# Reading the moving operand of a matmul by turns from its two halves, and adding shuffled sums into x with a step

## The chip, the cores and the metric

The kernel runs on 1 core of one Trainium2 chip. The metric is the device time of one execution in microseconds (us). Three runs of the kernel before the change gave 1353.87, 1353.93 and 1354.22 us; their median, 1353.93 us, is the time that the change is held against.

## What is computed

A trunk of four layers works on 256 tokens of width 1024, in float32. Each layer has a mixer (layers 0 and 3 an RWKV-7 mixer, layer 1 stick-breaking attention, layer 2 attention over selected keys), and after it a SwiGLU feed-forward part. Both add into the residual x. Cut to what the change touches:

```python
def swiglu(h, w_gu, w_down):
    g, u = jnp.split(h @ w_gu, 2, axis=-1)
    return (jax.nn.silu(g) * u) @ w_down

for i in range(DEPTH):
    h = rms_norm(x, norm_mix[i])
    ...
    x = x + y            # y = (mixer output) @ w_out, 1024 x 1024
    x = x + swiglu(rms_norm(x, norm_ffn[i]), ffn_w_gu[i], ffn_w_down[i])
return x
```

The feed-forward width is 2816, so one layer multiplies by two matrices of 1024 x 2816 (gate and up) and one of 2816 x 1024 (down).

## The kernel before

**Layout.** Everything is kept transposed: the 128 partitions hold features, the free axis holds the 256 tokens (S = 256). x lives in four tiles `xt[0..3]`, each with two chunks of 128 features, so eight chunks in all (NC = 8).

**Precision by parts.** The large products run in the format that the code calls F32R, four bytes an element. Each operand is split into a high part, which is the value cast to F32R, and a low part, which is the rest. The product is high x high + high x low + low x high. A weight piece of 512 KB (128 partitions x 1024 floats) is loaded by DMA into a `raw` tile; ScalarE (or VectorE) casts it to `wh`, and VectorE subtracts to get `wl` (`piece`). In the feed-forward part some pieces go to places of a tile named `wring` instead of `wh` and `wl`.

**Gate and up** (`gemm1`, called from `ffn`). The activation tile `xg` holds for each of the eight chunks the high part and behind it the low part, 256 columns each and next to one another. Per chunk there are two matmuls into one PSUM bank: `wh` against all 512 columns (high and low at once), and `wl` against the 256 columns of the high part. Columns 256 to 511 of the bank are then added to columns 0 to 255 (`add2`, a ScalarE copy and a VectorE addition). 22 such pieces for gate and 22 for up make 352 pairs of matmuls a layer. The sums are scaled by the reciprocal root mean square (`rstd_bcast`, which holds one value per token in every partition), go through silu, and their product is split again into `h`: high 256 columns, low 256 columns.

**Down** (the second half of `ffn`). For each of the eight output chunks m, 22 pairs of the same kind (512 columns, then 256 columns) are accumulated in one bank `dn`; two VectorE additions of 256 columns then add both halves of the bank into `xt`. That is 176 pairs a layer. In the last layer the last chunk is done in two banks, low parts first.

**Output products of the mixers** (`out_half`). For each of four pairs of chunks, 4 x 2 groups of three matmuls of 256 columns go into a bank `po`, and one VectorE addition of 512 columns adds it into `xt[j]`. It is called twice in each mixer: 192 matmuls a mixer.

**Order.** All operations are recorded and then issued in an order that is stored in the source as a table of numbers (`ORDER`), so every instruction has the line of the recording helper (L564); in the profile, groups are told apart by the names of their tiles. VectorE, ScalarE, TensorE and the DMA queue each work strictly in their stored order.

**Where a step already occurs.** Before the change no matmul reads its moving operand with a step between neighbouring elements: the innermost step is one element throughout. One small copy does: the tile `E` (in `rwkv`) is filled from `SB` by copies of 32 partitions x 512 elements whose innermost step is 128 elements, that is 512 bytes. A few of these run on ScalarE, a few on VectorE. A copy `XT<-XT` of 32 partitions x 1024 elements next to it reads runs of 32 neighbouring elements.

Of the kernel before, what the change touches and what calls it, by code (L numbers as in the profile page):

```python
# [16 lines left out]
F32R = mybir.dt.float32r  # L17
BF16 = mybir.dt.bfloat16
AF = mybir.ActivationFunctionType
ALU = mybir.AluOpType  # L20
# [4 lines left out]
P = 128  # L25
S = 256
D = 1024
NC = D // P
NF = 11
# [311 lines left out]
x=|C=_^-S9$_0-qF-xI@0F%_o6-  # L341
# [29 lines left out]
class Plan:  # L371
# [15 lines left out]
    def unit(self, at_once=1, ns=0.0):  # L387

        plan = self

        class Unit:
            def __enter__(self):
                plan.unit_op = Op("tensor")
                plan.unit_op.ns = ns

            def __exit__(self, *_):
                op, plan.unit_op = plan.unit_op, None
                op.cost /= at_once
                op.cost = op.ns or op.cost
                plan._add(op)  # L400

        return Unit()
# [63 lines left out]
    def after(self, op, preds):  # L466
        op.preds |= set(preds)
# [100 lines left out]
def trunk(ctx: ExitStack, tc: tile.TileContext, xT_in, vecs_in, wts, lora_in, consts_in, id32_in, outT, order, layers=None):  # L568
# [7 lines left out]
    pe, dve, act, pool, sp = (plan.queue(n) for n in ("tensor", "vector", "scalar", "gpsimd", "sync"))  # L576
    anye = plan.queue("any")
    unit = plan.unit

    def T(shape, group=None, name="t", dtype=F32):  # L580
        return plan.tile(sb, [P] + list(shape), dtype, group, name)

    def t1(name):
        return T([S], "t", name)
# [4 lines left out]
    def bank(name, group="ps"):  # L589
        return plan.tile(psum, [P, 512], F32, group, name, "psum")  # L590


    xt = [T([2, S], name=f"xt{j}") for j in range(4)]
    for j in range(4):
        sp.dma_start(xt[j], xT_in[:, 2 * j:2 * j + 2, :])
    onesr = T([P], name="ones", dtype=F32R)
# [42 lines left out]
    def f(ap):  # L639
        return ap.bitcast(F32)  # L640
# [22 lines left out]
    def mm3(out, w, x, start, stop):  # L663
        (wh, wl), (xh, xl) = w, x
        pe.matmul(out, wh, xh, start=start, stop=False)
        pe.matmul(out, wh, xl, start=False, stop=False)
        pe.matmul(out, wl, xh, start=False, stop=stop)

    def split(h, l, src):
        anye.copy(h, src)  # L670
        dve.tensor_tensor(l, src, f(h), op=ALU.subtract)

    def exact(out, w, x, hl):

        split(hl[0], hl[1], x)
        with unit():
            pe.matmul(out, w, hl[0], start=True, stop=False)
            pe.matmul(out, w, hl[1], start=False, stop=True)

    def v3(t, n):  # L680
        return t.rearrange("p (k m) -> p k m", k=n)

    def ab(t):
        return t.rearrange("p (a b) -> p a b", a=2)

    def flat(t):
        return t.rearrange("p a b -> p (a b)")

    def add2(t, o, eng=anye):

        eng.copy(t, o[:, S:])
        dve.tensor_tensor(t, o[:, :S], t, op=ALU.add)

    def gemm1(key, x, name, group="g", raw=None, parts=None):


        out = bank(name, group)
        wh, wl = [v3(t, NC) for t in piece(key, raw, parts)]
        for c in range(NC):
            with unit():  # L700
                pe.matmul(out, wh[:, c], flat(x[:, c]), start=(c == 0), stop=False)
                pe.matmul(out[:, :S], wl[:, c], x[:, c, 0], start=False, stop=(c == NC - 1))
        return out

    def gemm2(key, xs, name):
# [12 lines left out]
    def out_half(key, half, xs, after):  # L718

        for j in range(4):  # L720
            o = bank("po", "g")
            wh, wl = [v3(t, 4) for t in piece(key + (half, j))]
            for k in range(4):
                with unit():
                    for n in range(2):
                        sl = slice(n * P, (n + 1) * P)
                        mm3(o[:, n * S:(n + 1) * S], (wh[:, k, sl], wl[:, k, sl]), xs(k),
                            start=(k == 0 and n == 0), stop=(k == 3 and n == 1))
            dve.tensor_tensor(xt[j], xt[j], ab(o), op=ALU.add)
            if half == 1:  # L730
                after(j)

# [46 lines left out]
        dve.scalar_tensor_tensor(r, a, 1.5, r, op0=ALU.add, op1=ALU.mult)  # L779
        return r  # L780

    def rstd_bcast(summed=False):
        if summed:
            ss = nstate["ss"]
        else:
            ss, sq = bank("ss"), t1("ssq")
            anye.tensor_tensor(sq, nstate["acc"][:, 0], nstate["acc"][:, 1], op=ALU.add)
            exact(ss[:, :S], onesr, sq, [T([S], "t", "ssr", F32R) for _ in range(2)])
        return rsqrt_of(ss[:, :S], S, "rstd", 1.0 / D, eps_rms)

    def rstd_col(rs):
# [8 lines left out]
    def xg_of():  # L800
        x = nstate["xg"]
        return lambda c: (x[:, c, 0], x[:, c, 1])


    def ffn(layer, after):
        last = layer == subs[-1][1]
        x = nstate["xg"]
        rsb = None
        hs = [v.rearrange("p (i k a s) -> p i k a s", i=n, k=2, a=2)
              for v, n in ((T([4096], g, "h", F32R), 4) for g in ("SA", "SZ", "PR"))]  # L810

        ring = T([6, PIECE], "QC", "wring", F32R)

        def place(n):

            return {"parts": ring[:, n // 2 % 3::3] if n % 2 else None}

        for i in range(NF):
            gus = T([2, 2, S], f"s{6 + i % 2}", "gus")
            gs, us = gus[:, 0], gus[:, 1]  # L820
            since = len(plan.ops)
            for k in range(2):
                add2(gs[:, k], gemm1(("g", layer, 2 * i + k), x, "gate", **place(4 * i + k)), act if i >= 0 else anye)
            if i == 0:
                rsb = rstd_bcast()[:, None, :].to_broadcast([P, 2, S])
                plan.ops[-1].haste = HASTE
            dve.tensor_tensor(gs, gs, rsb, op=ALU.mult)
            act.activation(gs, gs, AF.Silu)
            for k in range(2):
                add2(us[:, k], gemm1(("u", layer, 2 * i + k), x, "up", "ps", **place(4 * i + 2 + k)), act if i >= 0 else anye)  # L830
            if i >= 1:
                plan.in_turn(since, "gate", "up")
            dve.tensor_tensor(us, us, rsb, op=ALU.mult)
            dve.tensor_tensor(us, us, gs, op=ALU.mult)
            h = hs[i // 4][:, i % 4]
            act.copy(h[:, :, 0], us)
            dve.tensor_tensor(h[:, :, 1], us, f(h[:, :, 0]), op=ALU.subtract)

        n, since = 0, len(plan.ops)
        for m in range(NC):  # L840
            if last and m == NC - 1:
                o = bank("dn", "g"), bank("dn", "ps")
                ws = {n // NC: (wh, wl)}
                for a in (1, 0):
                    for k in range(2 * NF):
                        i, h = n + k, hs[k // 8][:, k // 2 % 4, k % 2]
                        if i // NC not in ws:
                            ws[i // NC] = [v3(t, NC) for t in piece(("d", layer, i // NC))]
                        wh, wl = ws[i // NC]
                        with unit():  # L850
                            pe.matmul(o[a][:, :S], wh[:, i % NC], h[:, a], start=(k == 0), stop=(a == 1 and k == 2 * NF - 1))
                            if a == 0:
                                pe.matmul(o[a][:, :S], wl[:, i % NC], h[:, 0], start=False, stop=(k == 2 * NF - 1))
                    dve.tensor_tensor(xt[m // 2][:, m % 2], xt[m // 2][:, m % 2], o[a][:, :S], op=ALU.add)
                plan.in_turn(since, "dn")
                after(m // 2, 1)
                continue
            o = bank("dn", "g" if m % 2 else "ps")
            for k in range(2 * NF):
                if n % NC == 0:  # L860
                    wh, wl = [v3(t, NC) for t in piece(("d", layer, n // NC))]
                h = hs[k // 8][:, k // 2 % 4, k % 2]
                with unit():
                    pe.matmul(o, wh[:, n % NC], flat(h), start=(k == 0), stop=False)
                    pe.matmul(o[:, :S], wl[:, n % NC], h[:, 0], start=False, stop=(k == 2 * NF - 1))
                n += 1
            for a in range(2):
                dve.tensor_tensor(xt[m // 2][:, m % 2], xt[m // 2][:, m % 2], o[:, a * S:(a + 1) * S], op=ALU.add)
            if m == NC - 1:
                plan.in_turn(since, "dn")  # L870
            if last and m == NC - 2:
                after(m // 2, 0)
            elif m % 2:
                after(m // 2)
# [500 lines left out]
    def stick(layer, after):  # L1375
# [12 lines left out]
        for p in range(8):  # L1388
            q, k = qk_[:, p, 0], qk_[:, p, 1]
            add2(q, gemm1(("sq", p), x, "qk"))  # L1390
            add2(k, gemm1(("sk", p), x, "qk"))
            if p == 0:
# [388 lines left out]
```

## Time and profile before

| | |
|---|---|
| median of the runs | 1353.93 us |
| span of the profiled execution, first to last instruction | 1351.7 us |
| median less span | 2.2 us |
| mean granted TensorE clock | 1.000 |
| TensorE matmul busy | 1344.5 us, 99% |
| VectorE busy | 1129.5 us, 84% |
| ScalarE busy | 729.8 us, 54% |
| DMA, mean over the span | 164 GB/s |

The median run and the span differ by 2.2 us, which lies outside the first and last instruction. "PE" is TensorE's matmuls and "PEld" its loads of weights, "DVE" is VectorE, "ACT" ScalarE, "SP" the engine that issues the transfers. A matmul's duration in the profile (390 ns, say) is from its start to the end of its results and overlaps the next one. The time that a matmul takes out of the stream is read from the distance between starts, or from the length of a long run of matmuls divided by their number.

The eight large stages, in order of time: the RWKV mixer of layer 0 (to about 185 us), its feed-forward part (to 368), the attention of layer 1 (to 483) and its feed-forward part (to 667), the selected-key attention of layer 2 (to 803), its feed-forward part (to 987), the mixer of layer 3 (to 1165) and the last feed-forward part (to the end). Some names run into one another at the seams.

### The profile page before, as it was taken

How to read it: one execution, taken by the hardware profiler on the slowest of the kernel's cores; microseconds unless marked ns; L12 is line 12 of the kernel's file. 1: busy time of each engine (PE TensorE's matmuls, PEld its weight loads, DVE VectorE, ACT ScalarE, POOL GpSimd, SP SyncE). 2: the span in 40 equal slices, each digit the busy share in tenths (PEclk: the TensorE clock that was granted, in tenths of full speed). 3: DMA queues.
4: the chain of work that ended last, by engine and by line, in shares of the span. 5: the costliest groups of instructions: out<-in, count | busy, mean ns of one | idle time of the engine just before them, and what ended most of it. 6: DMA issues, size and time to landing. Idle time of an engine off the chain costs nothing.

```text
span 1351.7 us, 25734 instructions
## 1 busy us (share of the span) xinstructions
PE 1344.5 (99%) x10388; PEld 1183.0 (88%) x10388; DVE 1129.5 (84%) x1907; ACT 729.8 (54%) x1250; POOL 7.5 (1%) x18
## 2 busy tenths in 40 slices
PE   9999999999999999999999999999999999999998
PEld 8888898888888898888999798888898888988888
DVE  7998899876688899875899989876799997998754
ACT  4945545654344655554256865654148554656532
POOL 0000000000000000000000000000000000000000
PEclk9999999999999999999999999999999999999999
DMA  6422166654564456655646556666644231666554
GB/s 234 162 92 83 50 205 213 197 179 157 190 175 137 140 177 205 208 160 171 201 145 186 155 156 218 199 192 203 189 138 126 98 99 34 215 206 197 176 166 133
DMA packets 62999, 221.89 MB, mean 164 GB/s; under 512 B 7328, under 2 KB 8864, under 8 KB 62624
## 3 DMA queue, kind: packets, MB, share of 16 engines
q1 hardware_dynamic: 62880, 220.25, 52.2%
q8 instruction: 81, 1.33, 0.4%
q14 instruction: 38, 0.31, 0.1%
HBM read 217.08 MB, written 1.05 MB: 161 GB/s over the span
## 4 chain that ended last, share of the span: by engine, by line
PE 99%; DVE 1%; issue 0%; ACT 0%; DVEq 0%
PE gate L564 18%; PE up L564 18%; PE dn L564 18%; PE po L564 7%; PE qk L564 6%; PE vp L564 4%; PE rp L564 3%; PE kp L564 3%; PE vps L564 3%; PE z L564 2%; PE sc L564 1%; PE lora_in L564 1%; PE Y L564 1%; PE cmb L564 1%; PE pg L564 1%; PE attn_o L564 1%
## 5 line engine op out<-in xcount | busy, mean ns | idle before, releaser
L564 DVE TENSOR_TENSOR wl<-raw,wh 128x1024 fp32r<-128x1024 f32 x285 | 347.5, 1222 | 83.4 <-ACT wh L564 80.3
L564 ACT CAST wh<-raw 128x1024 fp32r<-128x1024 f32 x219 | 229.1, 1049 | 171.8 <-PE dn L564 92.8
L564 PE MATMUL dn<-h,wh 128*128 128x512 f32 (+1 forms) x726 | 244.3, 383 | 0.0
L564 PE MATMUL dn<-h,wl 128*128 128x256 f32 x704 | 198.1, 282 | 0.0
L564 PEld LDWEIGHTS dn<-h,wh 128*128 128x128 f32 x726 | 134.7, 188 | 26.9
L564 PE MATMUL up<-xg,wring 128*128 128x512 f32 x704 | 139.9, 336 | 0.0
L564 PE MATMUL gate<-xg,wring 128*128 128x512 f32 x704 | 138.3, 336 | 0.0
L564 PEld LDWEIGHTS dn<-h,wl 128*128 128x128 f32 x704 | 133.0, 189 | 0.0
L564 DVE TENSOR_TENSOR wring<-raw,wring 128x1024 fp32r<-128x1024 f32 x88 | 107.5, 1222 | 27.6 <-ACT wring L564 26.8
L564 PE MATMUL gate<-xg,wh 128*128 128x512 f32 x352 | 126.8, 392 | 0.0
L564 PE MATMUL up<-xg,wh 128*128 128x512 f32 x352 | 126.6, 392 | 0.0
L564 PEld LDWEIGHTS up<-xg,wring 128*128 128x128 f32 x704 | 107.5, 188 | 14.7
L564 PEld LDWEIGHTS gate<-xg,wring 128*128 128x128 f32 x704 | 107.4, 188 | 14.7
L564 ACT CAST wring<-raw 128x1024 fp32r<-128x1024 f32 x76 | 79.9, 1051 | 35.0 <-issue 13.5
L564 PE MATMUL gate<-xg,wl 128*128 128x256 f32 x352 | 98.4, 280 | 0.0
L564 PE MATMUL up<-xg,wl 128*128 128x256 f32 x352 | 98.4, 280 | 0.0
L564 PE MATMUL qk<-xg,wh 128*128 128x256 f32 (+1 forms) x384 | 91.5, 320 | 0.0
L564 PEld LDWEIGHTS up<-xg,wh 128*128 128x128 f32 x352 | 66.1, 188 | 14.5
L564 PEld LDWEIGHTS gate<-xg,wh 128*128 128x128 f32 x352 | 66.1, 188 | 14.4
L564 PE MATMUL qk<-xg,wl 128*128 128x256 f32 x256 | 71.6, 280 | 0.0
L564 ACT COPY gus<-gate 128x256 f32<-128x256 f32 x88 | 32.2, 372 | 71.7 <-PE gate L564 69.7
L564 PEld LDWEIGHTS qk<-xg,wh 128*128 128x128 f32 x384 | 63.6, 188 | 6.2 <-issue 0.5
(322 smaller groups left out, 2656.9 us busy)
## 6 DMA issues: line engine op xcount, KB each, us to landing
raw<-in_wts_dram SPq DMA_DIRECT2D x397, 512.0 KB, 3.8
lora<-in_lora_dram SPq DMA_DIRECT2D x2, 1536.0 KB, 10.6
rhl<-qa SPq DMA_DIRECT2D x32, 64.0 KB, 3.7
xt<-in_xT_dram SPq DMA_DIRECT2D x4, 256.0 KB, 4.1
lora<-in_lora_dram SPq DMA_DIRECT2D x2, 512.0 KB, 6.3
lg<-in_lora_dram SPq DMA_DIRECT2D x8, 128.0 KB, 4.4
inv<-in_id_dram SPq DMA_DIRECT2D x2, 512.0 KB, 3.9
out_dram<-xt SPq DMA_DIRECT2D x3, 256.0 KB, 3.7
```

Source lines behind the costliest of these rows:

```text
L564: getattr(getattr(nc, o.eng), method)(*map(real, args), **{k: real(a) for k, a in kw.items()})
```

## The change

Two new access patterns are brought in. `il` reads 256 columns as 0, 128, 1, 129, 2, 130, and so on: by turns from the first and the second half, with a step of 128 elements (512 bytes) between neighbouring reads. A matmul of 512 columns does that for its high 256 and then its low 256 columns. The matmul's output is written in order, as before, so the tokens stand shuffled in the bank.

- Gate and up (`gemm1` with `il`) read `xg` so. The reciprocal root mean square is made in the same shuffled order, by reading the moving operand of its own two matmuls with `il`; so the products between it, gate and up fit without more work. `h` is then in shuffled order.
- Down reads `h` with `il` once more, so its sums are shuffled twice.
- The output products of the mixers read their moving operand with `il`; their sums are shuffled once.
- The VectorE additions into `xt` undo this: they read the bank with a step of 2 elements (`po`) or 4 elements (`dn`) and write x in token order.

The query, key and value products, the RWKV products `kp`, `rp`, `vp` and the products `z` are left alone. The number, size and order of the instructions on every engine are the same in both programs; what differs is the access patterns, and the line numbers below the new helpers.

```diff
+    def il(t):
+
+        if len(t.cols.shape) == 2:
+            return t.rearrange("p a (q j) -> p a j q", q=2)
+        return t.rearrange("p (q j) -> p j q", q=2)
...
-    def gemm1(key, x, name, group="g", raw=None, parts=None):
+    def gemm1(key, x, name, group="g", raw=None, parts=None, il=lambda t: t if len(t.cols.shape) == 1 else flat(t)):
...
-                pe.matmul(out, wh[:, c], flat(x[:, c]), start=(c == 0), stop=False)
-                pe.matmul(out[:, :S], wl[:, c], x[:, c, 0], start=False, stop=(c == NC - 1))
+                pe.matmul(out, wh[:, c], il(x[:, c]), start=(c == 0), stop=False)
+                pe.matmul(out[:, :S], wl[:, c], il(x[:, c, 0]), start=False, stop=(c == NC - 1))
...
-                        mm3(o[:, n * S:(n + 1) * S], (wh[:, k, sl], wl[:, k, sl]), xs(k),
+                        mm3(o[:, n * S:(n + 1) * S], (wh[:, k, sl], wl[:, k, sl]), [il(x) for x in xs(k)],
...
-            dve.tensor_tensor(xt[j], xt[j], ab(o), op=ALU.add)
+            r = xt[j].rearrange("p n (q j) -> p n q j", q=2)
+            dve.tensor_tensor(r, r, o.rearrange("p (n j q) -> p n q j", n=2, q=2), op=ALU.add)
...
-            exact(ss[:, :S], onesr, sq, [T([S], "t", "ssr", F32R) for _ in range(2)])
+            exact(ss[:, :S], onesr, sq, [T([S], "t", "ssr", F32R) for _ in range(2)], il)
...
+    def quarters(t):
+        return t.rearrange("p (u v) -> p u v", u=4)
+
+    def quartered(o):
+        return o.rearrange("p (v u) -> p u v", u=4)
...
-                    pe.matmul(o, wh[:, n % NC], flat(h), start=(k == 0), stop=False)
-                    pe.matmul(o[:, :S], wl[:, n % NC], h[:, 0], start=False, stop=(k == 2 * NF - 1))
+                    pe.matmul(o, wh[:, n % NC], il(h), start=(k == 0), stop=False)
+                    pe.matmul(o[:, :S], wl[:, n % NC], il(h[:, 0]), start=False, stop=(k == 2 * NF - 1))
...
+            r = quarters(xt[m // 2][:, m % 2])
             for a in range(2):
-                dve.tensor_tensor(xt[m // 2][:, m % 2], xt[m // 2][:, m % 2], o[:, a * S:(a + 1) * S], op=ALU.add)
+                dve.tensor_tensor(r, r, quartered(o[:, a * S:(a + 1) * S]), op=ALU.add)
```

More of the change, by code (lines that the diff above doesn't have):

```diff
@@ L671, in split, with exact @@
         dve.tensor_tensor(l, src, f(h), op=ALU.subtract)
-    def exact(out, w, x, hl):
+    def exact(out, w, x, hl, il=lambda t: t):
         split(hl[0], hl[1], x)
         with unit():
-            pe.matmul(out, w, hl[0], start=True, stop=False)
-            pe.matmul(out, w, hl[1], start=False, stop=True)
+            pe.matmul(out, w, il(hl[0]), start=True, stop=False)
+            pe.matmul(out, w, il(hl[1]), start=False, stop=True)
     def v3(t, n):
@@ L780, in rsqrt_of, with rstd_bcast @@
         return r
-    def rstd_bcast(summed=False):
+    def rstd_bcast(summed=False, il=lambda t: t):
         if summed:
@@ L822, in ffn @@
             for k in range(2):
-                add2(gs[:, k], gemm1(("g", layer, 2 * i + k), x, "gate", **place(4 * i + k)), act if i >= 0 else anye)
+                add2(gs[:, k], gemm1(("g", layer, 2 * i + k), x, "gate", **place(4 * i + k), il=il), act if i >= 0 else anye)
             if i == 0:
-                rsb = rstd_bcast()[:, None, :].to_broadcast([P, 2, S])
+                rsb = rstd_bcast(il=il)[:, None, :].to_broadcast([P, 2, S])
                 plan.ops[-1].haste = HASTE
@@ L829, in ffn @@
             for k in range(2):
-                add2(us[:, k], gemm1(("u", layer, 2 * i + k), x, "up", "ps", **place(4 * i + 2 + k)), act if i >= 0 else anye)
+                add2(us[:, k], gemm1(("u", layer, 2 * i + k), x, "up", "ps", **place(4 * i + 2 + k), il=il), act if i >= 0 else anye)
             if i >= 1:
@@ L850, in ffn @@
                         with unit():
-                            pe.matmul(o[a][:, :S], wh[:, i % NC], h[:, a], start=(k == 0), stop=(a == 1 and k == 2 * NF - 1))
+                            pe.matmul(o[a][:, :S], wh[:, i % NC], il(h[:, a]), start=(k == 0), stop=(a == 1 and k == 2 * NF - 1))
                             if a == 0:
-                                pe.matmul(o[a][:, :S], wl[:, i % NC], h[:, 0], start=False, stop=(k == 2 * NF - 1))
-                    dve.tensor_tensor(xt[m // 2][:, m % 2], xt[m // 2][:, m % 2], o[a][:, :S], op=ALU.add)
+                                pe.matmul(o[a][:, :S], wl[:, i % NC], il(h[:, 0]), start=False, stop=(k == 2 * NF - 1))
+                    r = quarters(xt[m // 2][:, m % 2])
+                    dve.tensor_tensor(r, r, quartered(o[a][:, :S]), op=ALU.add)
                 plan.in_turn(since, "dn")
@@ L863, in ffn @@
                 with unit():
-                    pe.matmul(o, wh[:, n % NC], flat(h), start=(k == 0), stop=False)
-                    pe.matmul(o[:, :S], wl[:, n % NC], h[:, 0], start=False, stop=(k == 2 * NF - 1))
+                    pe.matmul(o, wh[:, n % NC], il(h), start=(k == 0), stop=False)
+                    pe.matmul(o[:, :S], wl[:, n % NC], il(h[:, 0]), start=False, stop=(k == 2 * NF - 1))
                 n += 1
+            r = quarters(xt[m // 2][:, m % 2])
             for a in range(2):
-                dve.tensor_tensor(xt[m // 2][:, m % 2], xt[m // 2][:, m % 2], o[:, a * S:(a + 1) * S], op=ALU.add)
+                dve.tensor_tensor(r, r, quartered(o[:, a * S:(a + 1) * S]), op=ALU.add)
             if m == NC - 1:
```

## The prediction, on record before the changed kernel ran

> **What bounds the kernel now.** First the page's busy shares and its chain, to see which engine sets the end; differences under 0.2% (2.7 us) count below as no change, about what a measurement of this kernel can tell.
>
> ```profile
> span 1351.7 us, 25734 instructions
> PE 1344.5 (99%) x10388; PEld 1183.0 (88%) x10388; DVE 1129.5 (84%) x1907; ACT 729.8 (54%) x1250; POOL 7.5 (1%) x18
> PE 99%; DVE 1%; issue 0%; ACT 0%; DVEq 0%
> PE gate L564 18%; PE up L564 18%; PE dn L564 18%; PE po L564 7%; PE qk L564 6%; PE vp L564 4%; PE rp L564 3%; PE kp L564 3%; PE vps L564 3%; PE z L564 2%; PE sc L564 1%; PE lora_in L564 1%; PE Y L564 1%; PE cmb L564 1%; PE pg L564 1%; PE attn_o L564 1%
> ```
>
> TensorE is the chain for 99% of the span, and the four products that the change touches (gate, up, dn, po) make up 61% of it. So what counts is how long one of their matmuls holds the stream. The chain in order of time gives that from long runs, one of each kind:
>
> ```profile
> 251.51 5.55 PE gate L564 x32
> 257.06 5.55 PE up L564 x32
> 306.98 61.03 PE dn L564 x352
> 1142.22 22.40 PE po L564 x192
> ```
>
> The second column is the length. Gate and up: 5.55 us for 16 pairs, 347 ns a pair. Down: 61.03 us for 176 pairs, 346.8 ns. Output: 22.40 / 192 = 117 ns a matmul of 256 columns. The timeline splits a pair:
>
> ```profile
> 251.70 0.39 PE L564 MATMUL gate<-xg,wh 128*128 128x512 f32 x1
> 251.93 0.28 PE L564 MATMUL gate<-xg,wl 128*128 128x256 f32 x1
> 252.04 0.39 PE L564 MATMUL gate<-xg,wh 128*128 128x512 f32 x1
> ```
>
> From start to start the 512 columns take 0.23 us and the 256 columns 0.11 to 0.12; with 347 for both and 117 from the output row, 230 and 117 ns. Is there anything in this that is not the columns themselves? Two other kinds of 256-column matmuls in this trace tell: the bfloat16 ones that warm the engine up, and the RWKV value product in plain float32.
>
> ```profile
> 6.13 0.49 PE L1615 MATMUL warm_o<-warm_x 128*128 128x256 bf16 x3
> 6.79 1.47 PE L1615 MATMUL warm_o<-warm_x 128*128 128x256 bf16 x12
> ...
> 89.83 1.46 PE L564 MATMUL vp<-xv,raw 128*128 128x256 f32 x6
> ```
>
> ```profile
> L564 PE MATMUL vp<-xv,raw 128*128 128x256 f32 x256 | 57.2, 381 | 0.0
> ```
>
> Three bfloat16 matmuls in a row take 0.49 us and twelve 1.47, so nine more are 0.98 us, 109 ns each. Six float32 ones, less the full duration of one (381 ns in the group's row): (1.46 - 0.38) / 5 = 216 ns, which is twice 108. So 256 columns at one column a beat need 108 to 109 ns, and 512 need 216 to 218. The F32R matmuls, which take four bytes at every beat, need 117 and 230: about 8 ns (256 columns) and 13 ns (512) more. That excess is absent where a column has two bytes (bfloat16) and where a column takes two beats (float32). It isn't the same for all F32R matmuls of one size either; the groups by form differ by the tile that is read:
>
> ```profile
> L564 PE MATMUL dn<-h,wh 128*128 128x512 f32 x682 | 236.9, 390 | 0.0
> L564 PE MATMUL gate<-xg,wh 128*128 128x512 f32 x352 | 126.8, 392 | 0.0
> L564 PE MATMUL vps<-wh,xg 128*128 128x512 f32 x128 | 42.5, 402 | 0.0
> ```
>
> 390, 392 and 402 ns mean for 512 columns out of `h`, `xg` and `wh`. So I read the excess as a stall of the moving operand's read at full rate, and one that depends on where and in which order the addresses come. The order is what the change alters; whether for better or worse this trace doesn't show, as no matmul in it reads with a step.
>
> **The change part by part.**
>
> *The reads of the four products.* Pairs: 4 layers x (352 gate and up + 176 down) = 2112. Output matmuls: 4 mixers x 192 = 768. Bounds on the good side: no excess left at all, a pair of 217 + 109 = 326 ns instead of 347, so 2112 x 21 = 44 us, and 768 x 8 = 6 us; together 50. A floor of another kind stands before that: the next weights have to be loaded within the matmul.
>
> ```profile
> 401.94 0.34 PE L564 MATMUL z<-ehl,ones 128*128 128x128 f32 x2
> 402.05 0.19 PEld L564 LDWEIGHTS qk<-xg,wh 128*128 128x128 f32 x1
> 402.16 0.19 PEld L564 LDWEIGHTS qk<-xg,wl 128*128 128x128 f32 x1
> ```
>
> Behind matmuls of only 128 columns (some 55 ns of columns) two weight loads still start 0.11 us apart, so a load takes about 110 ns of the stream. A 256-column matmul can't fall much under 111. I take 217 + 111 = 328 for the pair: 2112 x 19 = 40 us, and 768 x 6 = 4.6 us for the output.
>
> *Bounds on the bad side* come from the only reads with a step of 512 bytes in this trace, the copies into `E`:
>
> ```profile
> L564 ACT COPY E<-SB 32x512 f32<-32x512 f32 x11 | 12.0, 1090 | 8.3 <-DVE SB L564 8.1
> L564 ACT COPY XT<-XT 32x1024 f32<-32x1024 f32 x2 | 2.1, 1041 | 0.0
> L564 DVE COPY E<-SB 32x512 f32<-32x512 f32 x5 | 3.0, 595 | 0.1
> ```
>
> On ScalarE 512 elements with that step take as long as 1024 in runs (1090 against 1041): half rate. On VectorE they take 595 ns, some 1.1 ns an element. TensorE needs one every 0.42. At half rate a pair costs 2 x 326 = 652 ns: 2112 x 305 = +644 us, and 768 x 99 (216 for 117) = +76. At VectorE's pace a pair would take 768 x 1.1 = 845 ns and an output matmul 282, +1052 and +127 us.
>
> Between -50 and +1180 us I take the value near the good end. The reader of a stream at full rate must already fetch ahead, and the change doesn't alter how many different stretches of memory are read, only that two are open at once, each at half the speed; at half the speed per stretch, plain float32 shows no stall. That is an argument, not a row, and the chances below leave room for the other.
>
> *The additions into x with a step.* 64 and 32 of them:
>
> ```profile
> L564 DVE TENSOR_TENSOR xt<-xt,dn 128x256 f32<-128x256 f32 x64 | 26.6, 418 | 19.9 <-PE dn L564 19.1
> L564 DVE TENSOR_TENSOR xt<-xt,po 128x512 f32<-128x512 f32 x32 | 21.8, 683 | 1.0 <-PE po L564 0.7
> ```
>
> The nearest row with a step on VectorE is the copy into `E` above: 595 ns for 512 elements, less than the 683 here, although its step is far larger. So I take no cost; a gain is out, since one operand and the number of elements stay. Ceiling: half rate for the elements, 418 - 267 = 151 ns fixed, so +0.27 us each and +0.53 for the wide ones: 17 + 17 = 34 us of VectorE, most of it beside TensorE, but two narrow ones stand on the chain where a feed-forward part ends:
>
> ```profile
> 368.03 0.43 DVE xt L564
> 368.49 0.42 DVE xt L564
> ```
>
> That is 4 x 2 x 0.27 = 2 us of the end time at the ceiling.
>
> *The reciprocal root mean square* is two matmuls a layer for the feed-forward parts, a few ns each: nothing.
>
> *What is late next.* VectorE makes the low weights. If TensorE gets faster, VectorE has less time for them. Busy time by stretch (length, PE, PEld, DVE):
>
> ```profile
> 163.00:185.00 22.00, 22.00 (x189) 21.95 (x188) 21.19 (x35) 13.13 (x22) 0.00 (x0) 1.00 0.53 163
> 185.00:240.00 55.00, 55.00 (x320) 48.41 (x319) 53.18 (x79) 31.32 (x53) 0.00 (x0) 1.00 0.68 211
> 240.00:307.00 67.00, 67.00 (x388) 58.98 (x387) 52.54 (x74) 37.62 (x59) 0.00 (x0) 1.00 0.58 181
> 307.00:368.00 61.00, 61.00 (x353) 54.07 (x353) 38.71 (x50) 22.89 (x28) 0.00 (x0) 1.00 0.55 174
> ```
>
> In the second half of gate and up VectorE is at 78%, in down at 63%: room for a stream 5.5% shorter (63.3 and 57.7 us). In the first 55 us of the part it is at 97%: TensorE would need 52.0, VectorE has 53.2 of work there. So 1 to 2 us of the gain are given back in each of four feed-forward parts; I take 4 us in all. In the output product (163 to 185) VectorE is at 96%, so of the 4.6 us I count 2.
>
> Sum: -40 - 2 + 4 = -38 us. Against the profiled execution, 1351.7 becomes 1314; with the 2.2 us outside the span, 1353.9 - 38 = 1316 us.
>
> **The rivals.**
>
> *Only part of it* (0.20). The stall goes for the wide matmuls alone (2112 x 13 = 27 us), or half of it goes (20), or VectorE takes more back: 1328 to 1345, say 1334. For it: the weight floor of 110 is near 117, so the narrow ones may be bound by it already.
>
> *TensorE's pace doesn't change* (0.10). If the stall comes with the bytes and not with their order, the pairs stay at 347 and only the additions are left, 0 to 2 us on the chain: 1354 to 1356, a little more where VectorE is at 97%. Against it: 390 to 402 ns for the same bytes.
>
> *Every read opens a new line* (0.13). [...] It decides as soon as a column of the four products costs more than 347 / 768 = 0.45 ns on average. At half rate the time is 1353.9 + 644 + 76 = 2074 us, at VectorE's pace for such a step 2530. For it: the ScalarE row. Against it: VectorE reads the same pattern at a full element a beat, so the memory itself doesn't force half rate.
>
> [...]
>
> *A small loss* (0.05). The pace stays or gains little, and the additions cost their ceiling in the stretches where VectorE is at 96 to 97%: up to 34 us, 1358 to 1388.
>
> **How the numbers follow.** Forecast, most of the stall gone, 1302 to 1328: 0.52. Faster by over 0.2% is that and the partial case: 0.72. Within 0.2%: 0.07 of the 0.10 for no change of pace. Slower: 0.03 of it, 0.13 and 0.05: 0.21. The low end is 1353.9 - 50, with a little for the reading of the rows: 1302. The high end takes in the partial case, the unchanged pace and the first us of a loss: 1358. What is left out is the line case and most of the small loss, under 0.2.
>
> **What the changed profile would show.** In the chain, runs of 32 gate or up matmuls at 5.25 us (5.55 before) and the down stage at 57.7 (61.03); the mean of a 512-column matmul near 378 ns (390), a 256-column one near 274. Output runs of 192 at about 21.5 (22.40). The `xt` additions at 418 and 683 as before. VectorE over 97% and first TensorE waits for `wl` behind a feed-forward part's start. Wrong: runs of 32 at 5.55 (pace unchanged), or at 10 us and more (the line case, with VectorE's share near 50%); 256-column starts still 117 apart with wide ones shorter (the weight floor); `xt` rows near 690 and 1220.

## The result

The changed kernel takes 1314.39 us (median of four runs, 1313.07 to 1318.03) against 1354.08 for the kernel before (its three runs and a fourth, 1353.87 to 1355.63): a ratio of 0.9707, 95% interval 0.9692 to 0.9722, so 39.7 us or 2.9% less. The forecast was 1316 us. The profiled execution is the slowest of the four, 1318.03 us, with a span of 1316.3.

Page of the changed kernel: span, busy shares, and the chain by engine and by line.

```profile
span 1316.3 us, 25734 instructions
PE 1305.1 (99%) x10388; PEld 1168.9 (89%) x10388; DVE 1126.5 (86%) x1907; ACT 728.3 (55%) x1250; POOL 7.6 (1%) x18
PE 93%; DVE 3%; DMA 2%; ACT 1%; issue 1%; SPq 0%; DVEq 0%; ACTq 0%
```

VectorE's work is the same to 3 us; TensorE's got 39 us less. The chain now leaves TensorE for 7% of the span, where it was 1% before: others have begun to be late.

Chain in order of time, changed kernel (start, length, what): a run of gate, a run of up, a whole down stage, and a run of output products.

```profile
248.90 5.24 PE gate L564 x32
254.14 5.24 PE up L564 x32
...
462.54 10.92 PE po L564 x96
...
589.58 57.64 PE dn L564 x352
```

Gate and up went from 5.55 to 5.24 us for 16 pairs, 327.5 ns a pair; down from 61.03 to 57.64, 327.5 as well. The output products take 10.92 / 96 = 113.8 ns; the same stretch of 96 took 11.40 / 96 = 118.8 before (this row is from the kernel before):

```profile
471.88 11.40 PE po L564 x96
```

The timeline of the changed kernel shows both halves of a pair shorter, 0.21 to 0.22 and 0.11 from start to start:

```profile
245.03 0.27 PE L564 MATMUL up<-xg,wl 128*128 128x256 f32 x1
245.14 0.38 PE L564 MATMUL up<-xg,wh 128*128 128x512 f32 x1
245.35 0.27 PE L564 MATMUL up<-xg,wl 128*128 128x256 f32 x1
```

The groups by form say the same of the durations, and the additions into x with a step cost nothing (changed kernel; the last two rows are from the view of the tile `xt`, durations as minimum, median, maximum):

```profile
L564 PE MATMUL dn<-h,wh 128*128 128x512 f32 x682 | 223.9, 382 | 0.0
L564 PE MATMUL dn<-h,wl 128*128 128x256 f32 x704 | 191.6, 273 | 0.0
```

```profile
L564 DVE TENSOR_TENSOR xt<-xt,dn x64: 412/416/424, 308.7 to 1312.6; 128x256 f32<-128x256 f32 x64
L564 DVE TENSOR_TENSOR xt<-xt,po x32: 676/680/689, 166.9 to 1137.3; 128x512 f32<-128x512 f32 x32
```

What was not gained lies at the start of the feed-forward parts. Between the first gate and the first down matmul 352 pairs at 327.5 ns and two small ones need 115.5 us. By the starts of the first gate and the first down matmul, the first part took 184.52 to 306.82 us before (122.3) and 184.01 to 301.14 now (117.1); the four (117.1, 116.1, 116.8, 117.4) make 467.4 us where 462.0 would do, against 489.3 before. The chain of the changed kernel shows who is late there:

```profile
193.94 5.78 DMA raw<-in_wts_dram
...
199.74 1.05 ACT wh L564
...
203.23 1.23 DVE wring L564
204.45 0.04 issue
204.50 0.38 PE gate L564
```

A weight piece lands, ScalarE casts it, VectorE makes its low part, and only then TensorE goes on. In the view of waits TensorE waits for that by name, which it did nowhere before (total, times, longest):

```profile
PE gate L564 <- DVE wring L564: 0.8, 2, 0.6
```

VectorE's share in the first 56 us of the first feed-forward part is 96% (53.79 of 56.00 us; it was 97% of 55 us before):

```profile
184.00:240.00 56.00, 55.28 (x335) 50.00 (x334) 53.79 (x81) 32.27 (x55) 0.00 (x0) 1.00 0.69 211
```

### The profile page after: what moved, and what is told of

Same layout as the page of the kernel before. It is cut to its first block, busy times and chain, and to the rows that moved or that the text cites. A ratio compares the mean times of both kernels' runs of the same rounds, so it can differ in the third digit from the quotient of the medians.

```text
span 1316.3 us, 25734 instructions
## 1 busy us (share of the span) xinstructions
PE 1305.1 (99%) x10388; PEld 1168.9 (89%) x10388; DVE 1126.5 (86%) x1907; ACT 728.3 (55%) x1250; POOL 7.6 (1%) x18
## 4 chain that ended last, share of the span: by engine, by line
PE 93%; DVE 3%; DMA 2%; ACT 1%; issue 1%; SPq 0%; DVEq 0%; ACTq 0%
PE dn L564 17%; PE up L564 16%; PE gate L564 16%; PE qk L564 6%; PE po L564 6%; PE vp L564 4%; PE kp L564 4%; PE rp L564 3%; PE vps L564 3%; PE z L564 2%; DMA raw<-in_wts_dram 2%; DVE wl L564 1%; PE sc L564 1%; PE lora_in L564 1%; PE Y L564 1%; PE cmb L564 1%
## 5 line engine op out<-in xcount | busy, mean ns | idle before, releaser
L564 PE MATMUL dn<-h,wh 128*128 128x512 f32 (+1 forms) x726 | 230.9, 376 | 0.0
L564 PE MATMUL dn<-h,wl 128*128 128x256 f32 x704 | 191.6, 273 | 0.0
L564 PE MATMUL gate<-xg,wring 128*128 128x512 f32 x704 | 132.8, 328 | 1.3 <-DVE wring L564 0.8
L564 PE MATMUL up<-xg,wring 128*128 128x512 f32 x704 | 133.5, 327 | 0.2 <-DVE wring L564 0.2
L564 PE MATMUL gate<-xg,wh 128*128 128x512 f32 x352 | 121.5, 383 | 0.6 <-DVE xg L564 0.5
L564 PE MATMUL up<-xg,wh 128*128 128x512 f32 x352 | 120.8, 382 | 0.0
L564 PEld LDWEIGHTS up<-xg,wl 128*128 128x128 f32 x352 | 67.6, 192 | 0.3 <-DVE wl L564 0.3
```

The source lines that it names most:

```text
L564: getattr(getattr(nc, o.eng), method)(*map(real, args), **{k: real(a) for k, a in kw.items()})
```

## The experiments

The theory: reading neighbours one after another at full rate stalls the moving operand, and reading two places by turns doesn't; the rest of the kernel only takes a little of that back. The rivals: any shuffle would do; the distance between the halves matters; the stall is a collision with the load of the next weights; the gain is given back by what comes late.

### Ways of reading, measured alone

A kernel that copies x to the output and otherwise only runs 40 matmuls for each way of reading, with 128 x 128 weights, which change every time for F32R (shortened):

```python
("halves",   x[:, 0:256].rearrange("p (q j) -> p j q", q=2))
("quarters", ... q=4)  ("eighths", ... q=8)  ("step16" to "step2", ... q=16 to 128)
("turn2" to "turn32", x[:, 0:256].rearrange("p (q j r) -> p j q r", q=2, r=2 to 32))
("far16b" to "far128b", x[:, 0:256].rearrange("p (j q r) -> p j r q", q=2, r=4 to 32))
("far1k", "far4k", halves of 512 and 2048 elements, 256 columns of them)
```

> This kernel leaves the whole computation out (it copies x to the output) and runs 40 matmuls back to back for each way of reading the moving operand, with weights that change at every matmul, so that the distance between starts is the price of one matmul. If the stall belongs to reading neighbours in turn out of one stretch (my theory), 256 F32R columns in order cost 116 to 118 ns and by turns from two halves 109; more open places (quarters, eighths, steps of 16, 8 and 4 elements) stay at 109 too, and bfloat16 columns cost 109 either way. If two open places are just what a small line store can hold (rival: lines, but two of them), quarters and everything with more places cost more than 117, up to 216. If the shuffling matters only through the distance of the two places (rival: banks), turns at 16, 32, 64 and 128 bytes differ from turns at 512, 1024 and 4096 bytes. If any order that isn't plain neighbours will do, evens then odds (step 2) also costs 109; by my theory it stays at 115 or more, since it walks through one stretch at a time. The same element 256 times costs 109 if the stall comes from moving on to new memory.

Chain of this kernel, one row for each way of 40 (a number at the end of a name is left out by the view: the two `mrun` rows are 256 and 512 columns, the two `mhalves` rows likewise):

```profile
16.67 4.79 PE mrun L65 x40
21.46 4.47 PE mhalves L65 x40
25.93 5.50 PE mquarters L65 x40
31.43 8.93 PE meighths L65 x40
...
106.96 4.47 PE mfar4k L65 x40
111.43 4.47 PE mfar16b L65 x40
...
133.78 9.10 PE mrun L65 x40
142.87 8.63 PE mhalves L65 x40
...
169.01 4.38 PE mbfrun L65 x40
173.40 9.73 PE mbfhalves L65 x40
```

In order, 256 columns cost 120 ns, by halves 112, and 512 columns 227.5 against 215.8. The distance is of no importance: turns between two neighbouring groups of four elements (16 bytes apart) and between places 4 KB apart all cost 112, so the rival of distance falls. Four places cost 137 and eight 223, so "any shuffle" falls too. With it falls much of my own expectation, which had quarters, eighths and the steps of 16, 8 and 4 at 109: the steps of 16 and 8 came at 219 in the mean (17.30 us for 79), the step of 4 at 233. The rival with a store for just two open places had all of these above 117, and was right there. Evens, then odds, walks through one stretch at a time; my theory had it at 115 or more, near the price in order, and it costs twice that. The same element 256 times costs 112, like two places by turns. Cut out of the chain by a window, evens then odds, steps of four (second row) and runs of two by turns (third) read

```profile
66.97 9.08 PE mstep L65 x40
```

```profile
57.66 9.32 PE mstep L65 x40
```

```profile
76.28 6.33 PE mturn L65 x38
```

227, 233 and 167 ns; runs of 4 to 32 by turns cost 128 to 119 (5.11 us for 40, 4.88 for 41). And bfloat16, which I had at 109 either way, costs 243 by halves. So neither the number of stretches alone decides nor how often a new group of four neighbours comes up: in order and by turns between two places that is once in four columns alike, and the prices are 120 and 112. The order in which such groups come up counts, and it counts otherwise in bfloat16 (243 by halves, 109 in order).

### Columns, weights and steps, measured alone

The same frame, with 128 to 512 columns, 32 to 96 weight columns, weights with a step of 8 elements, both places moving on by 2, 4 or 16 elements, and shifted starts.

> This kernel leaves the whole computation out (it copies x to the output) and runs 40 F32R matmuls back to back for each case. In the first pattern run the excess over reading by turns was about the same for 256 columns (120 - 112) and for 512 (227.4 - 215.8), so there are two theories. Mine: the read in order stalls by itself, all along its columns; then the excess grows with the columns from 128 to 512 (by about 3 ns per 128 in order, against none by turns), and stays the same with 32, 64 or 96 weight columns. Rival: it stalls only while the next weights are being loaded, some 110 ns, because both read at once; then the excess is flat from 256 columns on, and shrinks in proportion to the weight columns (12 ns with 128, 3 with 32) with the widest gap for weights read with a step. By either, 128 columns cost about 110 ns with 128 weight columns (the load's own floor) and less with fewer. Two places that each move on by a step of 2 elements tell whether a place serves its neighbours: 112 if two places are enough, 120 or more if a line of 16 bytes has to give four columns in turn; with a step of 4 or 16 elements every read opens a new line: 220 or more. A start shifted by 1, 2, 3, 4 or 8 elements changes little (118 to 122).

Chain of this kernel (`cols` a is 128 columns, c 256, e 384, f 448, g 512; `weights_a` is 32 weight columns, `half` 256 and `full` 512 columns):

```profile
17.25 4.42 PE run_cols_a L66 x40
...
35.09 4.83 PE run_cols_c L66 x40
39.92 4.47 PE turn_cols_c L66 x40
...
55.69 6.94 PE run_cols_e L66 x40
62.63 6.50 PE turn_cols_e L66 x40
69.13 8.27 PE run_cols_f L66 x40
77.40 7.57 PE turn_cols_f L66 x40
...
102.68 4.55 PE run_half_weights_a L66 x40
107.23 4.37 PE turn_half_weights_a L66 x40
111.59 9.27 PE run_full_weights_a L66 x40
120.86 8.64 PE turn_full_weights_a L66 x40
...
192.62 9.61 PE turn_half_stepweights L66 x40
...
221.86 4.80 PE turn_evens L66 x40
226.66 9.07 PE turn_fours L66 x40
...
249.60 5.06 PE shift_two L66 x40
```

With 32 weight columns the excess of reading 512 columns in order is 231.8 - 216 = 16 ns; with 128 it was 11 or 12. So there the collision with the weights' load falls as the cause: a load of a quarter of the size leaves the excess. At 256 columns it doesn't fall altogether. By turns they stand on a floor set by the load: 112 ns with 128 weight columns, about what 128 columns cost (110.5), and 109 with 32. In order they cost 121 and 114. Over the 109, the excess is thus 12 ns with 128 weight columns and 4.5 with 32, near the 12 and 3 that the rival had, though not in proportion (4.5 with 64, 7 with 96). So the read in order has an excess of its own, and at 256 columns a part of it goes with the load.

My half of the expectation isn't borne out cleanly either: the excess doesn't grow evenly (9 ns at 256 columns, 11 at 384, 17.5 at 448, 11 at 512). A shifted start, which I had at 118 to 122, gives 117 (by 3, 4 and 8 elements) to 127 (by 2): the price of the read in order depends on where it starts, and the kernel's 117 lies in this range.

Both places moving on by two elements cost 120, just as much as reading in order; by four, 227, and by sixteen 224 (8.96 us for 40). So the gain is there where each place gives four neighbouring columns, 16 bytes, before it moves on (112, the turns 16 bytes apart above), and gone where each moves on by two elements.

An estimate from these numbers that fits most of them: count, for the even and for the odd columns apart, how often a new group of four elements comes up, and put 1.8 ns on each (227 / 128 for 512 columns in order). In order that is once in four columns, which makes 228 ns for 512 columns and 114 for 256 (231.8 and 114 measured with 32 weight columns); by turns it is once in eight, 114 ns for 512, less than the 215.8 that they take in any case. It fits evens (114 against 120), fours and eighths (227 against 227 and 223) as well. It doesn't fit quarters (137) nor runs of two (167), which it would put at 227, and 448 columns in order take 207 where it has 199. No run shows what stands behind the count; why the order of the reads matters stays open.

### One part of the change at a time

Three kernels, each with one product reading by turns: gate and up with their reciprocal root mean square (`il(h)` back to `flat(h)`, the step of the additions 2 in place of 4, `out_half` as before); down (`gemm1` without `il`, step 2); the output products (the rest as before).

> Only gate, up and their reciprocal root mean square read by turns; down and the output products read in order, and the additions into x undo one shuffle. The traces give 22 us less in the four gate and up stages (5.2 + 6.2 + 5.6 + 4.9) out of 27 that the pace alone would give (1408 pairs x 19.3 ns). My theory (a fixed gain per matmul, less what VectorE and the weight loads take back there): 1354 - 22 = 1332 us. Rival, that the stages share a budget so that the loss in gate and up comes from down and the output products running ahead of their weights: 1327 us, all of the 27.

Measured 1332.42 us (1329.79 to 1335.10), ratio 0.983 with interval 0.980 to 0.986. That is what the theory had, and the whole range lies above the rival's 1327. But two of the four runs had a granted clock of 0.995 and 0.996 (see the last section); the other two took 1329.79 and 1331.44. In the profile of the first of these the four stages take 465.3 us, 24 less than the 489.3 before. So 3.3 us over the 462.0 are given back here too, though down and the output products read in order, which speaks against the rival; the theory's 22 is some 2 us short.

> Only down reads by turns, of an h in token order. 704 pairs x 19.3 ns = 13.6 us; the traces show 3.4 us less in each of four down stages, which had VectorE at 63%, so nothing is taken back: 1354 - 13.5 = 1340.5 us. Rival (the stage is bound by the weight loads, 0.5 MB per 2.6 us): 1344 us or more.

Measured 1342.70 us (1340.59 to 1345.67), ratio 0.991, 0.988 to 0.994. Chain of this kernel:

```profile
602.14 57.64 PE dn L564 x352
```

The stages got their 3.4 us each, as in the full change; the median is 2 us above the forecast, and the best run on it. The profiled run, 1345.67 us, shows where some 5 us went in it: the clock (the last section). At 327.5 ns a pair these stages aren't held up by the weights' transfers, as the rival had it. So this part too is the fixed gain per matmul.

> Only the output products of the mixers read by turns. By the pace alone 768 matmuls x 4 to 8 ns = 3 to 6 us less, 1348 to 1351 us. My theory after seeing the traces: VectorE has 96% work there, the mixers as a whole got only 0.4 us shorter, so 1353.5 us, not to be told from 1354.

Measured 1351.35 us (ten runs, 1350.43 to 1356.09), ratio 0.998, 0.997 to 0.9997. I had it at nothing; alone it brings 2.6 us by the medians, and by the interval 0.4 to 4.2. In the profiles the 768 matmuls are busy for 92.08 us where they read by turns (changed kernel) in place of 95.45, so the pace gives 3.4 us; whether VectorE takes any of that back, these runs can't tell. Chain of this kernel, to 11.40 before:

```profile
471.10 10.92 PE po L564 x96
```

### More open places in the kernel itself

`q=2` becomes `q=4` in `il` and the additions, `u=4` becomes `u=16`.

> The changed kernel, with turns between four quarters in place of two halves (step 64 elements) and the additions into x undoing that. My theory (two open places are read at full rate, four are not): from the patterns alone, 137 ns for 256 columns in place of 112, and twice that for 512, so pairs of 411 ns in place of 327.5: 2112 x 84 = +176 us, and 768 x 24 = +18, about 1508 us. Rival (in the kernel's own mix any shuffle will do): 1314.

Measured 1546.36 us (one run). Chain of this kernel:

```profile
340.46 75.11 PE dn L564 x352
```

A pair takes 427 ns (411 worked out from the patterns; 2112 x 16 ns = 34 of the 38 us above the forecast), so the same kernel with a slightly different shuffle is 14% slower than reading in order. The gain is that of two places, not of shuffling.

### Who takes back the rest

```diff
-            dve.tensor_tensor(gs, gs, rsb, op=ALU.mult)
+            dve.tensor_tensor(gs[:, :, :16], gs[:, :, :16], rsb[:, :, :16], op=ALU.mult)
...
-            dve.tensor_tensor(us, us, gs, op=ALU.mult)
+            dve.tensor_tensor(us[:, :, :16], us[:, :, :16], gs[:, :, :16], op=ALU.mult)
```

> The changed kernel with less work for VectorE in gate and up: the scaling of gate and the product of gate and up are done for 16 of 256 columns of each chunk only (the rest of the output is left wrong), 1.2 us less VectorE work in each of the 44 groups of four pieces. My theory, that VectorE's work on the low weights takes back the missing 6 us in gate and up: the four stages, 117.1, 116.1, 116.8 and 117.4 us, come down to about 115.5 each, 1314 - 5 = 1309 us. Rival, that the weight transfers are late by themselves in the first 40 us of each feed-forward part (the chain has one of 5.8 and one of 5.5 us there): stages and total unchanged, 1314.

The changed kernel was run again beside it:

> The changed kernel again, on the chip of these runs, as the line for the other three: 1314 us, between 1313 and 1318.

Measured 1313.79 us (1312.20 to 1316.24) with less work for VectorE, and 1315.12 (1314.50 to 1316.86) for the changed kernel. VectorE's busy time fell from 1126.5 to 1087.1 us, and the time by 1.3 us where I expected 5; the ranges overlap. In the profiles the first gate and up stage is 299.64 - 183.82 = 115.8 us against 301.38 - 184.72 = 116.7 in the changed kernel's repeat, and its chain there is TensorE alone; but all four stages together are 464.5 against 465.6 us. VectorE's load is thus a part of it at most; how much the landing of the weights does by itself stays open.

### The other products by turns as well

```diff
-mm3(out[:, i * S:(i + 1) * S], (wh[:, c % 4, sl], wl[:, c % 4, sl]), xs(c),
+mm3(out[:, i * S:(i + 1) * S], (wh[:, c % 4, sl], wl[:, c % 4, sl]), [il(x) for x in xs(c)],
...
-add2(q, gemm1(("sq", p), x, "qk"))
+add2(q, gemm1(("sq", p), x, "qk", il=il), turned=True)
...
-pe.matmul(o[tb], xh[:, tsl], wh[:, c % 2, :], start=(c == 0), stop=False)
+pe.matmul(o[tb], xh[:, tsl], il(wh[:, c % 2, :]), start=(c == 0), stop=False)
```

`kp` is treated alike, and the reads of the banks get the step that undoes it.

> The changed kernel, with the remaining F32R products read by turns as well: the query, key and value products of both attentions, and rp and kp of the RWKV mixers; their banks are read back with a step of 2 (by VectorE, and by ScalarE where it copies). By the pace alone: 1272 matmuls of 256 columns x 6 ns = 7.6 us, 128 pairs x 19 ns = 2.4, 192 value matmuls of 512 columns x 16 ns = 3; 13 us below the changed kernel's 1314, so 1301. My theory: the mixers have VectorE at 88 to 97%, so about half of it comes through, 1307 us (1303 to 1311). Rival: ScalarE's and VectorE's reads with a step from PSUM cost as much as they gain, 1314 or more.

Measured 1309.42 us (1308.41 to 1313.78), ratio to before 0.9674, 0.9656 to 0.9693, and 5.7 us under the changed kernel's 1315.12 beside it: faster than both. Chain of this kernel, and then of the changed kernel's repeat:

```profile
364.23 10.58 PE vps L564 x48
375.99 14.14 PE qk L564 x86
```

```profile
365.75 11.41 PE vps L564 x48
378.35 14.96 PE qk L564 x86
```

So 44% of the 13 us by pace came through, within the range expected. That VectorE's load in the mixers took the rest was not tested. Reads of a bank with a step of 2 took as long as without on both engines, so the rival falls: ScalarE's copies from `kp` take 602 against 609 ns and from `qk` 372 in both, VectorE's additions from `qk` 418 against 420. ScalarE's row for `kp` in this kernel:

```profile
L564 ACT COPY k<-kp 128x512 f32<-128x512 f32 x7 | 3.9, 602 | 1.2 <-PE kp L564 1.2
```

## Why the prediction was right

**The bound.** TensorE's stream set the end (99% of the chain before, 93% in the changed kernel), and the price of a matmul in it was what counted. Each of the three parts made alone shortened just its own stages.

**The excess as a stall of the read.** The step that carried the sum, that F32R columns in order cost more than columns by turns, was inferred from rows of other formats and stood without a row of its own. The patterns show it: 120 against 112, 227.5 against 215.8. The reasoning beside it, that two stretches open at once halve the speed of each, holds only in part: by the same reasoning quarters and eighths should have gained too, and they cost 137 and 223 ns; and that the reader fetches ahead is shown by no run. That the change reads two places and not four, which would have made the kernel 14% slower, was luck as far as this argument goes.

**The pair.** Worked out 328 ns, measured 327.5; 2112 x 19.3 = 41 us, against 40. The patterns measured alone add up to it on both sides: 227.5 + 120 = 347.5 ns before and 215.8 + 112 = 327.8 now. The floor by the weights' load, about 110 ns, is there where narrow matmuls follow one another: 128 columns cost 110.5 ns, 256 by turns 112.

**The output products.** 111 ns worked out, 113.8 measured, and 3.4 us by the pace where I had 4.6 and counted 2. Alone it brings 2.6 (0.4 to 4.2). That was right in size; less came from the pace than I had, and that VectorE takes part of it is not shown.

**The additions with a step.** No cost, as taken: 416 and 680 ns against 418 and 683. The ceiling of 34 us was far off. No row shows its 267 ns for 256 elements as it stands; the two rows give 683 - 418 = 265.

**What is given back.** 4 us in the feed-forward starts; the profiles show 5.4 (467.4 - 462.0) in the slowest run and 3.6 (465.6 - 462.0) in the repeat. The place was right: the first TensorE waits for `wring` are there. VectorE's share there is 96%, not over 97%. The cause that I named, VectorE's work on low weights, is at most a part of it, as less of that work gave back some 1 us.

**The rivals.** Not only the wide matmuls gained: those of 256 columns went from 282 to 273 ns in down, and from 118 to 109 from start to start (medians over the trace), so the weights' floor didn't bind them within a pair, and the pace did change. The line case that would have made it 2074 us or more didn't come in for two places. For four it came in part (quarters, 1546 us), and eight cost twice the price (223 ns). No run shows how the reader keeps what it has read, in lines or otherwise; the runs show what an order costs. By turns, where every read is on another group of four elements than the one before, 256 F32R columns cost 112 ns, less than the 120 in order; evens, then odds, which read two elements of a group and then go on to the next, cost 227; and in bfloat16 halves cost 243 against 109. The trace of before couldn't decide that rival, and 0.13 left room for it.

## What to carry to other kernels

Where TensorE is busy all the time, hold the distance between starts against another format's of the same number of columns: an excess of a few per cent in every matmul is worth as much as a long stall (here 347 against 327.5 ns a pair, 39.7 us in all), and a change of the read order may remove it. For F32R with a run of columns as the moving operand, two places by turns did (120 to 112 ns for 256 columns, 227.5 to 215.8 for 512); the shuffle cost nothing here, where the next step is per column and the last one reads the bank with a step (additions of 416 and 680 ns against 418 and 683). Measure the very pattern and format alone first: four places (137 ns), or two in bfloat16 (243 against 109), cost far more than was gained here.

## What was not expected of the hardware

- For 256 F32R columns, two places by turns cost 112 ns from 16 bytes to 4 KB apart, four 137 and eight 223, and reading in order 117 to 127 by where it starts; in bfloat16 two places already cost 243 against 109.
- Weights read with a step of 8 elements make a 256-column matmul take 240 ns (9.61 us for 40) in place of 112. 512 columns take hardly more, 242 (9.68 us for 40), so the columns hardly count; that the weights' load is then the bound is inferred from that.
- The granted clock fell in the middle of a busy kernel. In the profiled run with down alone its mean was 0.57 over 12 us in the last mixer's chain of small matmuls, which by an estimate costs some 5 us (12 x 0.43); that run took 1345.67 us, the other three, at 1.000, 1340.59 to 1343.68. The window in that run (length, PE, PEld, DVE, ACT, POOL, granted clock, DMA share, GB/s):

```profile
1106.00:1118.00 12.00, 11.88 (x244) 9.90 (x242) 4.93 (x12) 1.87 (x5) 0.00 (x0) 0.57 0.01 3
```

The granted clock falls to 0.57 there although TensorE counts as busy (11.88 of 12.00 us); it does mostly small matmuls of 32 and 64 columns. The profiled run with quarters has such a stretch too (0.57 from 1256 to 1268 us; its mean clock is 0.997, so by the same estimate some 5 of its 193 us more are the clock's). It doesn't come with the change: one of the runs of the kernel before took 1360.83 us at a mean clock of 0.996. Nor do the small matmuls alone bring it: in the profiled run of the kernel before, the last mixer's chain ran at 1.00 (1112 to 1124 us). Two runs with gate and up alone, one with the output products alone and one with the other products by turns show 0.995 or 0.996 too. Why some executions meet it is open.
